# One hybrid encoder block: all big weights packed on the host in 8 KB pieces, full-row low parts of k, and projections emitted half a head sooner

## The chip, the cores and the metric

The kernel runs on one core of a Trainium2 chip. The metric is device time of one execution in microseconds (us); smaller is better. Repacking the weights is done with numpy before the launch and is not part of it.

## The reference, cut to what matters

Everything is float32. One sequence of 512 tokens, 1024 features, 16 heads of 64, 32 experts of width 512.

```
h = rmsnorm(x, norm_mix_g)
cb, cc, cu, q, k, v, f_logit, g_conv, g_att = split_cols(h @ w_in)     # w_in: 1024 x 8208
y_conv = short_conv(cb, cc, cu, conv_w, conv_b) @ w_conv_out
s = q k^T / sqrt(64) + cum[t] - cum[s]       # cum: running sum of log_sigmoid(f_logit + b_forget), causal
o = softmax(s) v                             # per head
m = sigmoid(g_conv) * y_conv + sigmoid(g_att) * (o @ w_att_out)
x = x + m @ w_out
x = x + hier_moe(rmsnorm(x, norm_ffn_g))     # best of 4 groups, then top 2 of its 8 experts
out = rmsnorm(x, norm_final_g)               # expert: (silu(h Wg) * (h Wu)) Wd
```

## The kernel before, in words

**Precision.** A float32 product is made of three fast TensorE products: both operands are split into a high part (a rounded copy, made by ACT) and a low part (the rest, made by DVE), and high x high, high x low, low x high are summed in PSUM. `mm3` (its matmuls are L120) does this over 8 blocks of 128 input features, 24 matmuls in all; `split` (L83 on ACT, L84 on DVE) makes the parts of a weight.

**Weights.** Projection weights come in column chunks of 256 (`CW`), 1 MB each. `load_raw` (L98) loads a chunk on SP's queue into one of two buffers (`wraw`), as `[128 partitions, 8 row blocks, 256 columns]`: each of a partition's eight pieces is 1 KB of DRAM, from another row of the weight. `split_w` then writes halves of the chunk into five buffers (`whl`). A `wraw` buffer is free for the next load when both halves are split, so each engine's queue and these two buffers set when a load starts.

**Stages.**
1. Start (written in the order of issue): x is normed and transposed into `hT`. The columns of v for the first four heads and the 16 of the forget gate come as two halves (`raw_v`, L245 and L246), q and k of these heads follow (`raws0`). The forget gates go through a chain of small DVE steps (`f_acc`), a transpose (`pf`, L391) and a running sum into DRAM (`ncd`), from where each head reads its row as `nct`.
2. Attention: per head `scores` (per block of 128 queries two products, L466 and L467, and a mask, L468; then DVE L469, the exponent on ACT L475), `transp` (L491) and `pvmm` (L507). Between heads, `gen_units` supplies 18 units of projection work (q, k, v of the next four heads; each 24 matmuls of 512 columns or the like) and `NSG` = 3 units of the attention gate (`pga`). A scheduler sets the order in each engine's queue from this program order. A pair of heads shares tiles: `q` holds for head r its own high part on the head's 64 rows and the low part on the other 64; `khi` holds the high part on both halves. `klo` holds the low parts of the pair, each on its own 64 rows, so L467 takes 64 of the 128 rows of both operands.
3. Merge: `gated` and the conv branch, all `mm3` with 512 columns; for the first `NSG` feature blocks the gate is already there.
4. Output projection (`px`), router and norm, woven by hand; `gain_rows` writes the normed tokens in a column order that suits the expert weights' rows, and they are stored in DRAM (`h2d`) and gathered by expert (`xg`).
5. Experts: gate and up (`pg`, L1022), down (`py`, L1037), combine (`pk`, L1063). Weights are loaded once each, 192 pieces of 1 MB, into 17 buffers (`prefetch`, L671) as buffers come free; a partition's piece is 8 KB of DRAM already, the next partition's lying 16 KB further.
6. Final norm and stores.

Of the kernel before, what the change touches and what calls it, by code (L numbers as in the profile page):

```python
# [13 lines left out]
F32 = mybir.dt.float32  # L14
F32R = mybir.dt.float32r
# [9 lines left out]
P = 128  # L25
T = 512
D = 1024
NK = D // P
# [16 lines left out]
def block_kernel(ctx, tc, x, norm_mix_g, w_in, conv_w, conv_b, b_forget, w_conv_out,  # L45
                 w_att_out, w_out, norm_ffn_g, w_router_group, w_router_expert,
                 w_e_gate, w_e_up, w_e_down, norm_final_g, out, dbg=None):
# [48 lines left out]
    def load_raw(src, name):  # L96
        raw = wraw.tile([P, NK, CW], F32, tag="wraw", name=f"raw_{name}")
        nc.sync.dma_start(raw, src.rearrange("(k p) f -> p k f", p=P))  # L98
        return raw

# [86 lines left out]
    qk = {}  # L187
# [7 lines left out]
    def qk_out(nm, pair, ps):  # L195
# [20 lines left out]
    def proj_qk(g):  # L216
        for nm, c0 in (("q", COL_Q), ("k", COL_K)):
            w = load_w(w_in[:, c0 + g * CW:c0 + (g + 1) * CW], f"{nm}{g}")
# [9 lines left out]
    with tc.tile_pool(name="s0", bufs=2) as s0:  # L228
# [6 lines left out]
        with tc.manual_schedule():  # L235
# [6 lines left out]
            for i in range(2):  # L242
                raw = p_tile(f"raw_v{i}")[:, 0:HK * VW].rearrange("p (k f) -> p k f", k=HK)
                src = w_in[i * T:(i + 1) * T].rearrange("(k p) f -> p k f", p=P)
                nc.sync.dma_start(raw[:, :, 0:CW], src[:, :, COL_V:COL_V + CW])  # L245
                nc.scalar.dma_start(raw[:, :, CW:VW], src[:, :, COL_F:COL_F + NH])  # L246
# [7 lines left out]
            raws0 = {nm: load_raw(w_in[:, c0:c0 + CW], nm + "0") for nm, c0 in (("q", COL_Q), ("k", COL_K))}  # L254
# [147 lines left out]
    NSG = 3  # L402
    sgp = opool.tile([P, NSG, T], F32, name="sgp")

    def gate_units():

        for fb in range(NSG):
            if fb % 2 == 0:
                w = load_w(w_in[:, COL_GA + fb * P:COL_GA + fb * P + CW], f"ga{fb}")
# [12 lines left out]
    with attx:  # L422
# [7 lines left out]
        def proj_v(g):  # L430
            w = load_w(w_in[:, COL_V + g * CW:COL_V + (g + 1) * CW], f"v{g}")
# [20 lines left out]
        def scores(h):  # L452
            pair, r = h // 2, (h % 2) * DH
            rows = slice(r, r + DH)
# [6 lines left out]
            for qb in range(NTB):  # L461
# [5 lines left out]
                nc.tensor.matmul(ps[:, :n], q[rows, h % 2, qs], kl[rows, :n], start=False, stop=False)  # L467
# [92 lines left out]
    if True:  # L560
        mT = (mga.tile([P, NK, T], F32R, name="mT_hi"), mga.tile([P, NK, T], F32R, name="mT_lo"))
        with tc.tile_pool(name="mg", bufs=2, side="right") as mg, \
# [7 lines left out]
            def gated(w_src, src, col, last):  # L570
                for c in range(D // CW):
                    ls = [lambda: load_w(w_in[:, col + c * CW:col + (c + 1) * CW], f"g{col}_{c}"),
# [801 lines left out]
```

## Time and profile before

| | us |
|---|---|
| median of 3 runs (1142.25 to 1765.85) | 1142.63 |
| profiled execution, its own time | 1140.45 |
| its span | 1138.9 |
| PE busy in the span | 1078.6 |
| DVE busy | 590.6 |
| ACT busy | 384.3 |

The profile covers one execution; its own time is the span and 1.5 us around it. The time of a matmul in it runs to a modelled end and overlaps the next one's, so the distance from start to start tells what one costs TensorE, and a high busy share doesn't mean that it never waits.

### The profile page before, as it was taken

The page shows a single profiled execution, that of the slowest core. Times are in us where ns is not written, and L with a number is a line of the kernel's source. Part 1 is how long each engine was busy: PE and PEld are TensorE (multiplying, and loading weights), DVE is VectorE, ACT ScalarE, POOL GpSimd, SP SyncE. Part 2 cuts the span into 40 slices and gives each one's busy share as a digit, 9 for nine tenths or more (in the row PEclk, how much of TensorE's full clock was granted, in tenths as well). Part 3 has the DMA queues.
Part 4 walks back from the last instruction along what each step waited for, and adds up shares of the span by engine and source line. Part 5 has one row for each costly group of instructions (what it writes and reads, how often), then busy time and mean ns, then how long its engine had stood idle before and what let it go on. Part 6 is the DMA issues. An engine that isn't in the chain of part 4 may idle for free.

```text
span 1138.9 us, 13609 instructions
## 1 busy us (share of the span) xinstructions
PE 1078.6 (95%) x5237; PEld 687.6 (60%) x5237; DVE 590.6 (52%) x1165; ACT 384.3 (34%) x726; POOL 53.1 (5%) x62
## 2 busy tenths in 40 slices
PE   6969999999999999999999799999999999999992
PEld 4747877687888888888899433333333333443441
DVE  6458776667422454433434425555555555445455
ACT  3436765567222333222342222222222222212222
POOL 4000000000200000000001200000000000000002
PEclk8989999999999999999999799999999999999996
DMA  7572343333755945555394799999999999999981
GB/s 206 61 117 65 68 81 72 59 74 59 134 124 82 105 93 95 94 99 125 107 361 166 298 389 419 419 418 419 419 418 419 419 419 420 418 418 419 419 341 76
DMA packets 83717, 268.07 MB, mean 235 GB/s; under 512 B 7104, under 2 KB 53232, under 8 KB 59072
## 3 DMA queue, kind: packets, MB, share of 16 engines
q1 hardware_dynamic: 76624, 255.34, 68.2%
q10 hardware_dynamic: 4224, 6.89, 1.9%
q0 software_dynamic: 2800, 4.93, 1.3%
q8 instruction: 42, 0.69, 0.2%
q14 instruction: 27, 0.22, 0.1%
HBM read 267.10 MB, written 4.23 MB: 238 GB/s over the span
## 4 chain that ended last, share of the span: by engine, by line
PE 84%; DMA 9%; DVE 3%; ACT 2%; issue 1%; DVEq 0%; SPq 0%; ACTq 0%
PE pg L1022 19%; PE py L1037 9%; PE py L120 8%; PE pg L120 6%; PE pk L1063 6%; PE px L120 4%; PE pb L120 4%; PE pu L120 4%; PE pc L120 4%; PE psv L120 3%; PE psq L120 2%; PE psk L120 2%; DMA raw_v<-in_w_in_dram 2%; PE s L467 2%; DMA raw_u<-in_w_e_up_dram 2%; DMA raw_d<-in_w_e_down_dram 2%
## 5 line engine op out<-in xcount | busy, mean ns | idle before, releaser
L1022 PE MATMUL pg<-raw_u,XT 128*64 128x512 f32 x512 | 235.1, 602 | 1.6 <-DMA raw_u<-in_w_e_up_dram 1.6
L1022 PE MATMUL pg<-raw_g,XT 128*64 128x512 f32 x512 | 236.1, 603 | 0.0
L1064 DVE TENSOR_TENSOR m<-pk,m 128x512 f32<-128x512 f32 x256 | 159.3, 684 | 137.6 <-PE pk L1063 137.5
L1022 PEld LDWEIGHTS pg<-raw_g,XT 128*64 128x64 f32 x512 | 64.9, 137 | 105.6 <-issue 102.7
L1037 PE MATMUL py<-raw_d,hTe 128*64 128x512 f32 x512 | 116.9, 598 | 0.0
L1047 DVE TENSOR_TENSOR Y<-py,Y 64x512 fp32r<-64x512 f32 x62 | 42.7, 688 | 75.8 <-ACT Y L1046 75.8
L1046 ACT ACTIVATE Y<-py 64x512 fp32r<-64x512 f32 x62 | 36.7, 592 | 125.3 <-PE py L1037 102.0
L1217 ACT ACTIVATE ta<-pg,rsl 64x512 f32<-64x512 f32 x32 | 21.9, 683 | 169.1 <-PE pg L1022 169.1
L1022 PEld LDWEIGHTS pg<-raw_u,XT 128*64 128x64 f32 x512 | 65.4, 137 | 21.0 <-issue 10.5
L1063 PEld LDWEIGHTS pk<-Y,S 128*128 128x128 f32 x248 | 41.7, 188 | 57.2 <-issue 49.5
L1063 PE MATMUL pk<-Y,S 128*128 128x512 f32 x248 | 74.6, 422 | 1.6 <-DVE Y L1047 1.6
L1037 PEld LDWEIGHTS py<-raw_d,hTe 128*64 128x64 f32 x512 | 34.0, 136 | 66.7 <-issue 59.7
L120 PE MATMUL pg<-hT_hi,whl_g 128*128 128x512 f32 x208 | 66.1, 389 | 0.0
L120 PE MATMUL px<-whl_o,mT_hi 128*128 128x256 f32 x256 | 47.9, 288 | 0.0
L120 PEld LDWEIGHTS pg<-hT_hi,whl_g 128*128 128x128 f32 x208 | 39.0, 188 | 8.1
L120 PE MATMUL psq<-hT_hi,whl_q 128*128 128x512 f32 x128 | 43.6, 408 | 0.0
L475 ACT ACTIVATE P<-P,mx 128x128 f32<-128x128 f32 (+1 forms) x64 | 35.2, 552 | 24.2 <-DVE mx L471 24.1
L120 PE MATMUL psk<-hT_hi,whl_k 128*128 128x512 f32 x128 | 42.8, 401 | 0.0
L469 DVE CUSTOM_DVE_ANT_0 P<-s,nct 128x128 f32<-128x128 f32 (+1 forms) x64 | 30.6, 489 | 22.4 <-PE s L468 17.7
L120 PE MATMUL py<-tT_hi,whl_y 128*128 128x512 f32 x128 | 40.7, 389 | 0.0
L120 PE MATMUL pg<-hT_lo,whl_g 128*128 128x512 f32 x104 | 40.5, 389 | 0.0
L120 PE MATMUL py<-oT_hi,whl_y 128*128 128x512 f32 x128 | 40.4, 389 | 0.0
(284 smaller groups left out, 1963.6 us busy)
## 6 DMA issues: line engine op xcount, KB each, us to landing
raw_g<-in_w_e_gate_dram SPq DMA_DIRECT2D x64, 1024.0 KB, 19.9
raw_u<-in_w_e_up_dram SPq DMA_DIRECT2D x64, 1024.0 KB, 19.9
raw_d<-in_w_e_down_dram SPq DMA_DIRECT2D x64, 1024.0 KB, 19.9
raw_g<-in_w_in_dram SPq DMA_DIRECT2D x7, 1024.0 KB, 11.7
raw_q<-in_w_in_dram SPq DMA_DIRECT2D x4, 1024.0 KB, 11.6
raw_k<-in_w_in_dram SPq DMA_DIRECT2D x4, 1024.0 KB, 13.6
nct<-ncd ACTq DMA_DIRECT2D x16, 256.0 KB, 3.2
raw_y<-in_w_att_out_dram SPq DMA_DIRECT2D x4, 1024.0 KB, 5.2
```

The lines of the kernel that those rows point to most:

```text
L120: nc.tensor.matmul(ps, blk(lhs[a], k, lsl), blk(rhs[b], k, rsl), start=i == 0, stop=i == 3 * NK - 1)
L467: nc.tensor.matmul(ps[:, :n], q[rows, h % 2, qs], kl[rows, :n], start=False, stop=False)
L469: nc.vector.tensor_tensor_reduce(Pt[:, P_OFF[qb]:P_OFF[qb] + kw], ps[:, :kw], nct[:, :kw], 1.0, NEG, ALU.add, ALU.max, mx[:, qb:qb + 1])
L475: nc.scalar.activation(Pt[:, sl], Pt[:, sl], AF.Exp, bias=mx[:, qb:qb + 1], accum_out=sm[:, qb:qb + 1])
L1022: nc.tensor.matmul(ps[r:r + DH], XT[:, k, j], w[k // 4][:, k % 4], start=k == 0, stop=k == NK - 1)
L1037: nc.tensor.matmul(py[n * DH:(n + 1) * DH], hTt[:, f], raws[f // 2][:, f % 2, n * T:(n + 1) * T], start=f == 0, stop=f == 3)
L1046: nc.scalar.activation(Y[hi, ns], py[hi], AF.Copy)
L1047: nc.vector.tensor_sub(Y[lo, ns], py[hi], Y[hi, ns].bitcast(F32))
L1063: nc.tensor.matmul(ps, S[:, tb * P:(tb + 1) * P], Y[:, ns], start=True, stop=True)
L1064: nc.vector.tensor_add(x2[:, tb, ns], ps, x2[:, tb, ns])
L1217: nc.scalar.activation(a, pg[0:DH], AF.Silu, scale=rsl[:, e:e + 1])
```

## The change

- `_pack` rearranges `w_in`, the three square weights and the expert weights with numpy: by chunk, partition and feature block, so that every 1 MB load is one run of DRAM in which each partition has one piece of 8 KB. The two first halves of v and the forget gate become one array `w_v0f`, a load each (4352 bytes a partition) with no second load on ACT's queue. The three expert arrays become one, `w_e`; its rows are in plain order, so `gain_rows` and `transpose_h` no longer permute columns.
- `klo` becomes two fixed tiles of `[128, 2, 512]`; the other head's 64 rows are set to zero once by POOL, and the product that was L467 (now L480) takes all 128 rows. A tile is written again by the pair after the next.
- `NSG` goes from 3 to 2: one gate unit moves from the attention into the merge, and the chunk that was loaded for it alone (`raw_ga2`) goes.
- `needed` emits the units that head h + 2 needs before `pvmm(h)`, where they stood before `scores(h + 1)` of the next turn.

```diff
     def load_raw(src, name):
         raw = wraw.tile([P, NK, CW], F32, tag="wraw", name=f"raw_{name}")
-        nc.sync.dma_start(raw, src.rearrange("(k p) f -> p k f", p=P))
+        nc.sync.dma_start(raw, src.rearrange("p (k f) -> p k f", k=NK))
         return raw
...
+    def klo_tile(pair):
+
+        if pair < 2:
+            t = klos[pair] = att.tile([P, 2, T], F32R, name=f"klo{pair}", bufs=1)
+            for r in range(2):
+                nc.gpsimd.memset(t[(1 - r) * DH:(2 - r) * DH, r].bitcast(F32), 0.0)
+        else:
+
+            assert 2 * (pair - 2) + 1 in scored
+        return klos[pair % 2]
...
-            kl = att.tile([P, T], F32R, tag="klo", name=f"klo{pair}", bufs=3)
+            kl = klo_tile(pair)
...
-                nc.vector.tensor_sub(kl[own], ps[own], kh[own, r].bitcast(F32))
+                nc.vector.tensor_sub(kl[own, r], ps[own], kh[own, r].bitcast(F32))
...
-                nc.sync.dma_start(raw[:, :, 0:CW], src[:, :, COL_V:COL_V + CW])
-                nc.scalar.dma_start(raw[:, :, CW:VW], src[:, :, COL_F:COL_F + NH])
+                nc.sync.dma_start(raw, w_v0f[i].rearrange("p (k f) -> p k f", k=HK))
...
-    NSG = 3
+    NSG = 2
...
-                nc.tensor.matmul(ps[:, :n], q[rows, h % 2, qs], kl[rows, :n], start=False, stop=False)
+                nc.tensor.matmul(ps[:, :n], q[:, h % 2, qs], kl[:, h % 2, :n], start=False, stop=False)
...
+        def needed(h):
+
+            return 6 * (h // 4) - (0 if h // 2 % 2 else 3) if 4 <= h < NH else 0
+
         scores(0)
         for h in range(NH):
 
             share = [NU * (2 * h + i) // (2 * NH) for i in range(2)]
             if h + 1 < NH:
-                g, odd = (h + 1) // 4, (h + 1) // 2 % 2
-                run_units(max(share[0], 6 * g - (0 if odd else 3) if g else 0))
+                run_units(max(share[0], needed(h + 1), 6 * (h // 4) - 1))
                 scores(h + 1)
             transp(h)
-            run_units(max(share[1], 6 * (h // 4) - 1))
+            run_units(max(share[1], needed(h + 2)))
             pvmm(h)
...
+        NBK = {"g": 4, "u": 4, "d": 2}
+
         def chunk_ap(part, n, i):
-
-            src = w_e_down if part == "d" else w_e_gate if part == "g" else w_e_up
-            return src[ORDER[n]].rearrange("(p i k) f -> i p k f", p=P, i=2)[i]
+            return w_e[ORDER[n], 2 * "gud".index(part) + i].rearrange("p (k f) -> p k f", k=NBK[part])
...
-            nc.tensor.transpose(pt[:, f], h.rearrange("t (p k) -> t k p", k=4)[:, f], identf[:DH, :DH])
+            nc.tensor.transpose(pt[:, f], h[:, f * P:(f + 1) * P], identf[:DH, :DH])
```

On PE, before the first score block of head 10 (`psk5` is the k projection of its pair, `t9`, `o9`, `o8` are transposes and PV products of heads 9 and 8, `psq6` the q projection of pair 6). Before:

```order
L120 MATMUL psk5_1776<-hT_hi_88,whl_k2_1_1482 128x512
L491 MATMUL t9_0_1844<-identf_60,P9_1654 128x128 x4
L491 MATMUL t9_1_1851<-identf_60,P9_1654 128x128 x3
L120 MATMUL psq6_1888<-hT_hi_88,whl_q3_0_1882 128x512
L120 MATMUL psq6_1888<-hT_lo_89,whl_q3_0_1882 128x512
L507 MATMUL o9_1866<-PThi1_615,v4_1597 128x512
...
L507 MATMUL o9_1866<-PTlo1_616,v4_1597 128x384
L466 MATMUL s10_0_1814<-khi5_1801,q5_1458 128x256
L467 MATMUL s10_0_1814<-klo5_1802,q5_1458 128x256
```

In the changed kernel, at the same place:

```order
L124 MATMUL psk5_1761<-hT_hi_88,whl_k2_1_1468 128x512
L520 MATMUL o8_1793<-PThi0_613,v4_1596 128x512
...
L520 MATMUL o8_1793<-PTlo0_614,v4_1596 128x256
L504 MATMUL t9_0_1842<-identf_60,P9_1706 128x128 x4
L504 MATMUL t9_1_1849<-identf_60,P9_1706 128x128 x3
L124 MATMUL psq6_1943<-hT_hi_88,whl_q3_0_1937 128x512
...
L479 MATMUL s10_0_1812<-khi5_1786,q5_1458 128x256
L480 MATMUL s10_0_1812<-klo1_596,q5_1458 128x256
```

The k projection now ends a PV product earlier: head 8's whole `pvmm` stands between it and the scores that read it, where four products of head 9's stood.

On POOL, after the store of the running sums (`ncd`) at the end of the start. Before:

```order
L338 TENSOR_TENSOR xt3_110<-xt3_110,gmix_111 128x1024
L393 MEMSET zero_552 16x512
L396 DMA ncd_103<-ncum_554 16x512
L565 IOTA ioti_2659 128x512
L692 DMA gcol_4399<-in_norm_ffn_g_dram 128x8x1
```

In the changed kernel:

```order
L406 MEMSET zero_550 16x512
L409 DMA ncd_103<-ncum_552 16x512
L198 MEMSET klo0_561 64x512 x2
L198 MEMSET klo1_596 64x512 x2
L582 IOTA ioti_2621 128x512
```

Four fills of 64 partitions by 512 elements are queued behind the store; the first `klo` product of head 0 and that of head 1 wait for POOL.

On SP's queue, where the attention ends and the merge begins (`y7184` and `g7184` are chunks of `w_att_out` and of the attention gate). Before:

```order
L98 DMA raw_v3_2188<-in_w_in_dram 128x8x256
L98 DMA raw_ga0_2479<-in_w_in_dram 128x8x256
L98 DMA raw_ga2_2589<-in_w_in_dram 128x8x256
L98 DMA raw_y7184_0_2663<-in_w_att_out_dram 128x8x256
L98 DMA raw_y7184_1_2723<-in_w_att_out_dram 128x8x256
```

In the changed kernel:

```order
L98 DMA raw_v3_2128<-in_w_in_dram 128x2048
L98 DMA raw_ga0_2511<-in_w_in_dram 128x2048
L98 DMA raw_y7184_0_2625<-in_w_att_out_dram 128x2048
L98 DMA raw_g7184_1_2685<-in_w_in_dram 128x2048
L98 DMA raw_y7184_1_2693<-in_w_att_out_dram 128x2048
```

`raw_ga2` is gone, and the shapes show one run of 2048 elements a partition in place of 8 of 256.

## Rows read from the trace of the kernel before

**Rows 1.** The page, section 4: the chain that ended last, by engine.

```profile
PE 84%; DMA 9%; DVE 3%; ACT 2%; issue 1%; DVEq 0%; SPq 0%; ACTq 0%
```

**Rows 2.** Stretches: length; busy PE, PEld, DVE, ACT, POOL; clock; DMA share; GB/s.

```profile
73.60:286.00 212.40, 207.11 (x1130) 161.32 (x1130) 151.59 (x386) 132.27 (x302) 1.47 (x2) 0.99 0.37 73
286.00:574.00 288.00, 288.00 (x1273) 238.46 (x1272) 115.82 (x145) 83.54 (x99) 4.85 (x8) 1.00 0.58 108
700.00:1000.00 300.00, 299.97 (x1354) 118.06 (x1350) 157.48 (x253) 71.21 (x126) 9.90 (x10) 1.00 1.01 419
```

**Rows 3.** The chain of waits in order of time: start us, us, what.

```profile
44.01 18.64 DMA raw_k<-in_w_in_dram
...
189.74 10.13 DMA raw_v<-in_w_in_dram
...
280.78 5.22 PE pga L120 x23
...
1005.57 20.57 DMA raw_d<-in_w_e_down_dram
```

**Rows 4.** DMA issues: queue, count, KB each, median us from issue to landing.

```profile
raw_k<-in_w_in_dram SPq DMA_DIRECT2D x4, 1024.0 KB, 13.6
...
raw_y<-in_w_att_out_dram SPq DMA_DIRECT2D x4, 1024.0 KB, 5.2
```

**Rows 5.** Timeline of the start, 38 to 78 us: start, length, engine, line.

```profile
62.68 1.06 ACT L83 ACTIVATE whl_k<-raw_k 128x1024 fp32r<-128x1024 f32 x1 [5.39 <-DMA raw_k<-in_w_in_dram]
...
66.33 1.02 PE L391 MATMUL pf<-identf,f_acc 128*16 128x128 f32 x4 [11.50 <-DVE f_acc L387]
```

**Rows 6.** Timeline of the first 25 us.

```profile
14.78 0.66 ACT L325 ACTIVATE PThi<-raw_v 128x544 fp32r<-128x544 f32 x1 [0.97 <-DMA raw_v<-in_w_in_dram]
...
17.37 4.65 POOL L338 TENSOR_TENSOR xt<-xt,gmix 128x1024 f32<-128x1024 f32 x2
...
17.46 2.27 DVE L146 SCALAR_TENSOR_TENSOR rs_t<-rs_y,rs_h 128x1 f32<-128x1 f32 x1
...
21.96 0.52 POOL L393 MEMSET zero<- 16x512 f32 x1
22.07 0.75 DVE L275 SCALAR_TENSOR_TENSOR xt<-xt,rstd,gmix 128x512 f32<-128x512 f32 x1
```

**Rows 7.** Timeline of PE, score blocks of one head.

```profile
150.26 0.36 PE L466 MATMUL s<-khi,q 128*128 128x256 f32 x1
150.55 0.38 PE L467 MATMUL s<-klo,q 64*128 64x256 f32 x1
150.86 0.23 PE L468 MATMUL s<-maskb,identb 128*128 128x128 bf16 x1
150.90 0.48 PE L120 MATMUL psq<-hT_hi,whl_q 128*128 128x512 f32 x1
...
151.89 0.47 PE L466 MATMUL s<-khi,q 128*128 128x512 f32 x1
152.29 0.50 PE L467 MATMUL s<-klo,q 64*128 64x512 f32 x1
152.73 0.23 PE L468 MATMUL s<-maskb,identb 128*128 128x128 bf16 x1
```

**Rows 8.** Timeline of PE, PV products of a head and a projection.

```profile
159.56 0.40 PE L507 MATMUL o<-PThi,v 128*128 128x512 f32 x1
159.80 0.40 PE L507 MATMUL o<-PTlo,v 128*128 128x512 f32 x1
...
161.31 0.28 PE L507 MATMUL o<-PThi,v 128*128 128x256 f32 x1
161.43 0.39 PE L120 MATMUL psk<-hT_lo,whl_k 128*128 128x512 f32 x1
```

**Rows 9.** Timeline, 195 to 206 us: what PE waits for at head 10.

```profile
199.89 1.06 ACT L83 ACTIVATE whl_v<-raw_v 128x1024 fp32r<-128x1024 f32 x1 [3.94 <-DMA raw_v<-in_w_in_dram]
...
201.61 0.39 PE L466 MATMUL s<-khi,q 128*128 128x256 f32 x1 [3.87 <-ACT khi L213]
```

More of the change, by code (lines that the diff above doesn't have):

```diff
@@ L97, in load_raw, with w_cols @@
         raw = wraw.tile([P, NK, CW], F32, tag="wraw", name=f"raw_{name}")
-        nc.sync.dma_start(raw, src.rearrange("(k p) f -> p k f", p=P))
+        nc.sync.dma_start(raw, src.rearrange("p (k f) -> p k f", k=NK))
         return raw
+    def w_cols(col):
+        return w_in[(col if col < COL_F else col - NH) // CW]
     def split_w(raw, name):
@@ L217, in proj_qk @@
         for nm, c0 in (("q", COL_Q), ("k", COL_K)):
-            w = load_w(w_in[:, c0 + g * CW:c0 + (g + 1) * CW], f"{nm}{g}")
+            w = load_w(w_cols(c0 + g * CW), f"{nm}{g}")
             for pair in (2 * g, 2 * g + 1):
@@ L253, in block_kernel @@
                 nc.sync.dma_start(xs[tb], x[tb * P:(tb + 1) * P])
-            raws0 = {nm: load_raw(w_in[:, c0:c0 + CW], nm + "0") for nm, c0 in (("q", COL_Q), ("k", COL_K))}
+            raws0 = {nm: load_raw(w_cols(c0), nm + "0") for nm, c0 in (("q", COL_Q), ("k", COL_K))}
             nc.scalar.dma_start(bfb, b_forget.rearrange("(o h) -> o h", o=1).to_broadcast([P, NH]))
@@ L408, in gate_units @@
             if fb % 2 == 0:
-                w = load_w(w_in[:, COL_GA + fb * P:COL_GA + fb * P + CW], f"ga{fb}")
+                w = load_w(w_cols(COL_GA + fb * P), f"ga{fb}")
             ps = psp.tile([P, T], F32, tag="proj", name=f"pga{fb}")
@@ L430, in proj_v @@
         def proj_v(g):
-            w = load_w(w_in[:, COL_V + g * CW:COL_V + (g + 1) * CW], f"v{g}")
+            w = load_w(w_cols(COL_V + g * CW), f"v{g}")
             v_tiles(g)
@@ L452, in scores @@
         def scores(h):
-            pair, r = h // 2, (h % 2) * DH
-            rows = slice(r, r + DH)
+            pair = h // 2
+            scored.append(h)
             q, (kh, kl) = qk["q", pair], qk["k", pair]
@@ L609, in block_kernel @@
                 for nm, col in (("c", COL_C), ("u", COL_U), ("b", COL_B)):
-                    w = load_w(w_in[:, col + c * CW:col + (c + 1) * CW], f"{nm}{c}")
+                    w = load_w(w_cols(col + c * CW), f"{nm}{c}")
                     for j in range(2):
@@ L739, in gain_rows @@
                 eng = nc.gpsimd if tb >= 2 else nc.vector
[L741 to L743 removed]
+                eng.tensor_mul(h2s[tb][:, c0:c1], x2[:, tb, c0:c1], gffn[:, c0:c1])
             def store_rows(tb):
@@ L1345, in block_kernel, with _pack, cols @@
             nc.sync.dma_start(out[tb * P:(tb + 1) * P], ot)
-_INS = ["x", "norm_mix_g", "w_in", "conv_w", "conv_b", "b_forget", "w_conv_out", "w_att_out", "w_out",
-        "norm_ffn_g", "w_router_group", "w_router_expert", "w_e_gate", "w_e_up", "w_e_down",
-        "norm_final_g"]
+_INS = ["x", "norm_mix_g", "w_in", "w_v0f", "conv_w", "conv_b", "b_forget", "w_conv_out", "w_att_out", "w_out",
+        "norm_ffn_g", "w_router_group", "w_router_expert", "w_e", "norm_final_g"]
 _OUTS = [((1, 512, 1024), "float32")]
+def _pack(inputs):
+    a = {n: np.asarray(v) for n, v in inputs.items()}
+    def cols(w):
+        return w.reshape(NK, P, -1, CW).transpose(2, 1, 0, 3).reshape(-1, P, NK * CW)
+    w = a["w_in"]
+    a["w_in"] = cols(np.concatenate([w[:, :COL_F], w[:, COL_GC:]], axis=1))
+    v0f = np.concatenate([w[:, COL_V:COL_V + CW], w[:, COL_F:COL_GC]], axis=1)
+    a["w_v0f"] = v0f.reshape(2, NK // 2, P, CW + NH).transpose(0, 2, 1, 3).reshape(2, P, NK // 2 * (CW + NH))
+    for n in ("w_conv_out", "w_att_out", "w_out"):
+        a[n] = cols(a[n])
+    a["w_e"] = np.concatenate([v.reshape(32, 2, v.shape[1] // 256, P, v.shape[2]).transpose(0, 1, 3, 2, 4)
+                               .reshape(32, 2, P, NK * CW) for v in (a["w_e_gate"], a["w_e_up"], a["w_e_down"])],
+                              axis=1)
+    return a
 def kernel(**inputs):
```

34 lines of the change are left out of this document (14 added, 20 removed).

## The prediction, made before the changed kernel ran

> **What bounds the kernel now.** I read the chain that ended last first: 84% of the span is PE and 9% DMA [rows 1], so each stage has to be asked what PE waits for there. The busy time by stretch comes next [rows 2]. In the merge PE is busy 288.00 of 288 us: its loads are hidden, whatever they cost. In the experts DMA is at 1.01 of its 16 engines and 419 GB/s for 300 us on end, and late in the stage the chain waits for `raw_d` [rows 3]: this stage ends when the stream of weights ends, and the stream starts when the stage before frees its buffers. The stage therefore moves as a block with whatever comes before it, and a faster TensorE inside it is worth nothing. In the attention PE shows 207.11 of 212.40 us, but starts, not ends, tell what a matmul costs, so the third view is the timeline of PE. The fourth is the chain in order of time, for the places where a load is waited for: `raw_k` for 18.64 us from 44.01 and `raw_v` for 10.13 us from 189.74 [rows 3].
>
> **The start: loads in 8 KB pieces.** A 1 MB chunk of `w_in` in 1 KB pieces lands after a median of 13.6 us, one of `w_att_out`, also in 1 KB pieces, after 5.2 [rows 4]. In the merge 0.58 of the DMA engines moves 108 GB/s, in the experts 1.01 moves 419 [rows 2]: 1 MB costs all engines 0.58 / 108 GB/s = 5.4 us there and 2.4 us here. The pieces of the experts are those that every weight gets now, so I take a landing between 2.4 us (that rate, no latency) and 5.2 us.
>
> From 38 to 67 us ACT splits chunks of the next group early; before `whl_k` it stands 5.39 us until that chunk lands [rows 5]. The splits are early work, but they stand in ACT's and DVE's queues ahead of the forget gates' small steps; these end 3.65 us after `raw_k` landed (62.68 to 66.33), and PE sits idle 11.50 us until then. `raw_k` is issued at 44.01, when its buffer is free. With 5.2 us it lands at 49.2 and `pf` could start at 49.2 + 3.65 = 52.9; PE gets there at 66.33 - 11.50 = 54.8 in any case. The whole wait of **11.5 us** goes, at either end of the landing, and what is late next is PE's own work.
>
> In the first 25 us ACT's split of the second half of v waits for its load until 14.78. Behind it POOL's two products with the gain run 4.65 us from 17.37, and DVE's tiny norm step beside them takes 2.27 us; the scaled second block of x, which PE waits for, starts at 22.07 [rows 6]. With v landing before 11, POOL's work starts up to 4.6 us sooner, and DVE's steps with it; but these still meet POOL's products, only earlier. Between 0 and 5 us; I take **3**, the middle, since half of DVE's delay is that meeting.
>
> **The attention: full-row low parts of k.** In a block of 256 columns L467 starts 0.29 us after L466 and L468 0.31 us after L467; with 512 columns it is 0.40 and 0.44 [rows 7]. A PV product with full rows and the same columns is followed by the next matmul after 0.12 us (256) and 0.24 us (512) [rows 8]. So each half-row product costs itself and its neighbour: 0.29 + 0.31 - 0.24 = 0.36 us in a small block, 0.40 + 0.44 - 0.48 = 0.36 in a large one. There are 16 heads x 4 blocks = 64 of them: 23 us. The mask product starts 0.04 us before its successor now (150.86 to 150.90, rows 7 again); alone, its 128 columns would cost half of 0.12, so about 0.02 us a block, or 1.3 us, comes back. **-21 us** with some rounding down for blocks whose L466 is fed late anyway. That the two rows stand apart only because of the 64 rows is an inference: operands, widths and clock are alike, and rows are what differs.
>
> The Trainium skill speaks on both sides here. "TensorE: Matmul & The Clock Gate", section "Why this matters for your kernels", says that a product with few rows takes the time of one with 128: by that, L467 loses nothing by its 64 rows, and the sum would be 21 us poorer. "TensorEngine Tiling (Array Packing)", section "Key Properties", says that a change of tiling mode drains the engine; by that the sum stands. The starts agree with the second: 0.29 and 0.31 us where 0.12 is had.
>
> Second term: at head 10 PE waits 3.87 us for `khi`, which stands in ACT's queue behind the split of `raw_v`, and that waited 3.94 us for its load [rows 9]. The load was issued at 189.74; with 5.2 us it lands at 194.9 in place of 199.9, and the wait goes. The granted clock over the attention is 0.99 [rows 2]; the 2.1 us (1% of 212.4) that this costs come from such waits, and most of it returns. **-5.4 us**.
>
> Third: the gate unit. 24 matmuls at 5.22 / 23 = 0.227 us [rows 3] leave the attention and stand in the merge, which PE bounds: -5.4 and +5.4, nothing. `raw_ga2` with its split goes with no one waiting for it.
>
> Fourth: what becomes late when PE is faster. DVE is busy 151.59 us and ACT 132.27 us of 212.4 [rows 2]; of a stage of 212.4 - 21 - 5.4 - 5.4 = 180.6 us DVE's work would be 84%. It is no bound by itself, but PE feeds two score buffers, and the next block must wait for DVE's pass over the block before the last. I put back 4 us: between 0, since the scheduler has projections to fill in, and 17 (below). The earlier emission works on the same account: the order shows head 8's whole PV product between k's projection and the scores of head 10, which covers ACT and DVE there; it is in the 4.
>
> The fills of `klo` on POOL stand behind the store of the running sums; a fill of 16 x 512 takes 0.52 us [rows 6], four make 2.1 us. PE's next work after `pf` is a k projection of 24 matmuls, 5.4 us, before any score reads `klo`: hidden. If `pf` came later than that projection they would cost up to 2.1 us. `klo`'s reuse waits for scores that stand more than one head earlier in PE's queue: nothing.
>
> **The experts.** Pieces stay 8 KB, now end to end. The stream already fills the engines, so I take 0. Its 192 pieces of 1.05 MB take 480 us at 419 GB/s; the 17 that fit ahead make 43 us of that, so 437 us have no cover, and bounds of 1% either way are 4 us. `gain_rows` and `transpose_h` in plain order act inside a stage that its stream bounds: 0.
>
> **How the numbers follow.** The profiled execution took 1140.45 us. Less 11.5, 3, 21 and 5.4, plus 4: 1140.45 - 36.9 = 1103.6 us. The median of the runs is 2.2 us above the profiled execution, so **1106 us**, 3.2% below the median. Verdicts at 2% start at 1119.8 us.
>
> **Rivals.**
> - DVE and ACT take over the attention (or the half rows are not the cause). For it: their busy share there grows from 71% to 84% of the stage, in queues that cannot skip ahead. Against it: PE is busy 207.11 of 212.40 us today [rows 2], and 3.87 of the rest are the one wait at head 10. Then the 21 us shrink to what they hide now; with 17 us given back, 1106 + 17 - 4 = **1119**; if the half rows cost nothing at all, 1106 + 21 - 4 = 1123.
> - The loads stay slow. `w_att_out` with 1 KB pieces lands in 5.2 us, so size alone isn't what makes `w_in` slow; it may be something that packing leaves. Then 11.5, 3 and 5.4 us stay where they are: 1106 + 19.9 = **1126**. Against it: the expert chunks have just this form and move at 419 GB/s. The Trainium skill, "DMA: Bandwidth & Descriptors", section "Specifications", puts the smallest transfer for full rate at 512 bytes: by it 1 KB pieces had nothing to gain. The share of 0.58 for 108 GB/s says otherwise.
> - Everything that waits goes too: no 4 us given back, 5 us in the first stretch, and the earlier emission removes short waits of PE before group changes, some 8 us: 1106 - 4 - 2 - 8 = **1092**.
> - The other side: the packed expert array streams more slowly than the three arrays did. The order of addresses can matter: chunks of `w_in` and `w_att_out`, equal in piece size, differ 13.6 to 5.2 us [rows 4]. With 437 us of stream uncovered, the 37 us gained are used up when it loses 37 / 437 = 8.5%; at 20%, which is far less than those two differ, it is 87 us longer, 1106 + 87 = **1193**. Against it: 1.01 of the engines for 300 us says that the engines, not the memory behind them, set the pace, and runs of 1 MB are not harder to read than pieces 16 KB apart.
>
> Chances: my forecast 0.58, DVE and ACT 0.19, slow loads 0.08, everything goes 0.11, slower stream 0.04. The range 1090 to 1122 takes in the first, most of the second and the fourth. About 2% is what a measurement of this kernel can tell from no change. Faster by more than that: 0.58 + 0.11, over half of the second (0.12) and a little of the third: 0.82. Slower: 0.03, as some of the last case stays near the median. The rest, 0.15, is the same.
>
> **What the new profile would show.** `pf` starts with no wait behind `raw_k`, before 55 us. `raw_k` and its like land in under 5.5 us. The starts of L479, L480 and L481 stand 0.12 to 0.13 us apart at 256 columns. The stretch from the first score to the last gate unit is near 186 us, DVE over 80% of it. The experts still run at 419 GB/s and as long as before. I would be wrong if the low product still starts 0.3 us after its neighbour, if PE waits for DVE between score blocks, or if the stream's rate is no longer 419.

## The result, and the profile after

The changed kernel takes **1111.95 us** (median of 4 runs, 1110.17 to 1112.66); the kernel before, on the same chip, 1144.66 (median of 4; one of them, of 1765.85, is far from every other and is left out of the ratio, which stands on the other three, 1142.25 to 1146.68). The ratio is 0.972, 95% interval [0.969, 0.975]: 2.8% faster. The forecast was 1106, its range 1090 to 1122. The profiled execution took 1110.17 us, its span is 1108.6; the sum of the prediction for that execution was 1103.6.

Stage by stage, between the same starts on PE in both timelines:

| From - to | before, us | after, us | change | predicted |
|---|---|---|---|---|
| span's start - first `psq` | 38.2 | 36.7 | -1.6 | -3 |
| first `psq` - `pf` | 28.1 | 16.5 | -11.7 | -11.5 |
| `pf` - first score | 7.3 | 5.9 | -1.4 | 0 |
| first score - first `py` of the merge | 212.2 | 190.3 | -21.9 | -27.8 |
| merge, to the first `px` | 288.3 | 294.7 | +6.4 | +5.4 |
| first `px` - end | 564.7 | 564.5 | -0.2 | 0 |
| sum | | | -30.3 | -36.9 |

The first row is one execution against one: in the nine runs whose start is that of the changed kernel the first `psq` comes between 36.6 and 37.7 us, 37.05 in the mean. Some 0.8 us of the merge's +6.4 come from the stage ahead of it: the granted clock is at its lower level, 1.2 GHz, from 247.8 to 251.1 us, behind the idle times of PE shown below, and the merge starts at 249.3. In experiment 4, without that idle time, the merge takes 293.9.

The windows of after stand beside [rows 2]: attention, merge, and 300 us of the experts (columns as there).

```profile
59.00:249.00 190.00, 183.66 (x1104) 153.42 (x1103) 146.96 (x379) 131.77 (x302) 0.00 (x0) 1.00 0.25 84
249.00:544.00 295.00, 295.00 (x1299) 244.24 (x1298) 116.50 (x150) 84.51 (x100) 6.34 (x9) 1.00 0.29 101
660.00:960.00 300.00, 298.30 (x1352) 117.72 (x1348) 157.56 (x253) 71.14 (x126) 10.87 (x11) 1.00 1.01 419
```

In the merge the DMA engines are taken for 0.29 of the time at 101 GB/s, where it was 0.58 at 108. The experts still stream at 419 GB/s. In the attention PE is idle for 6.3 us, and this idle time is in a new place. The landings, from the page's list of DMA issues (last number: median us), answer to [rows 4]:

```profile
raw_g<-in_w_in_dram SPq DMA_DIRECT2D x7, 1024.0 KB, 4.7
raw_k<-in_w_in_dram SPq DMA_DIRECT2D x4, 1024.0 KB, 5.5
...
raw_y<-in_w_att_out_dram SPq DMA_DIRECT2D x4, 1024.0 KB, 4.7
```

The chunks of `w_in` land in 4.7 (`raw_g`) and 5.5 us (`raw_k`, which took 13.6). At the start this does what [rows 5] let expect; here is the timeline of after around `pf`, ACT first, then PE:

```profile
48.36 1.05 ACT L83 ACTIVATE whl_k<-raw_k 128x1024 fp32r<-128x1024 f32 x1
...
52.88 0.39 PE L124 MATMUL psk<-hT_hi,whl_k 128*128 128x512 f32 x1
53.10 0.60 PE L404 MATMUL pf<-identf,f_acc 128*16 128x128 f32 x4
```

No row has a bracket, which would name a wait: nobody waits. PE comes to `pf` straight from a projection, and the four transposes take 0.60 us where they took 1.02 after the wait. The granted clock was 0.79 from `pf` to the first score before (66.3 to 73.6 us): its lower level, 1.2 GHz, until 69.3, behind PE's 11.5 us of idle time, and the upper one, 2.4 GHz, from there. It is 1.00 in that stretch now: that is the 1.4 us which the sum didn't have.

The first 25 us, for [rows 6]:

```profile
14.60 0.64 ACT L338 ACTIVATE PThi<-raw_v 128x544 fp32r<-128x544 f32 x1
...
15.14 1.04 ACT L279 ACTIVATE sq<-xt 128x1024 f32<-128x1024 f32 x1
...
16.09 0.19 ACT L279 ACTIVATION_READ_ACCUMULATOR sq<-xt 128x1 f32 x1
...
16.35 4.82 POOL L351 TENSOR_TENSOR xt<-xt,gmix 128x1024 f32<-128x1024 f32 x2 [1.94 <-DMA raw_q<-in_w_in_dram]
16.57 2.32 DVE L156 SCALAR_TENSOR_TENSOR rs_y<-rs_t,rs_y 128x1 f32<-128x1 f32 x1
18.93 2.26 DVE L150 SCALAR_TENSOR_TENSOR rs_t<-rs_y,rs_h 128x1 f32<-128x1 f32 x1
...
21.43 0.75 DVE L288 SCALAR_TENSOR_TENSOR xt<-xt,rstd,gmix 128x512 f32<-128x512 f32 x1
```

ACT's split of v no longer waits, but POOL's products begin only 1.0 us sooner (16.35 for 17.37). Before, they stood right behind POOL's own work on v, which ended at 17.41:

```profile
15.55 1.86 POOL L293 TENSOR_TENSOR PTlo<-raw_v,PThi 128x544 fp32r<-128x544 f32 x1
```

Now that work ends at 14.41, and POOL waits 1.94 us more. The bracket names `raw_q`, whose event came last, but the products don't read it. They overwrite blocks 2 and 3 of x, which had landed by 12.8 and 14.1 us; what ends just ahead of them, at 16.28, is ACT's square of block 2 (15.14, L279), which reads that block and stands in ACT's queue behind the split of v. DVE's one-column steps meet them as before, 2.3 us each, and the scale that PE waits for moves from 22.07 to 21.43.

The score blocks, for [rows 7], in the timeline of PE:

```profile
127.70 0.28 PE L479 MATMUL s<-khi,q 128*128 128x256 f32 x1
127.82 0.27 PE L480 MATMUL s<-klo,q 128*128 128x256 f32 x1
127.94 0.23 PE L481 MATMUL s<-maskb,identb 128*128 128x128 bf16 x1
127.98 0.36 PE L479 MATMUL s<-khi,q 128*128 128x256 f32 x1
128.18 0.28 PE L480 MATMUL s<-klo,q 128*128 128x256 f32 x1
128.30 0.23 PE L481 MATMUL s<-maskb,identb 128*128 128x128 bf16 x1
128.34 0.48 PE L124 MATMUL psq<-hT_hi,whl_q 128*128 128x512 f32 x1
128.66 0.34 PE L479 MATMUL s<-khi,q 128*128 128x384 f32 x1
128.84 0.33 PE L480 MATMUL s<-klo,q 128*128 128x384 f32 x1
129.02 0.23 PE L481 MATMUL s<-maskb,identb 128*128 128x128 bf16 x1
129.06 0.50 PE L479 MATMUL s<-khi,q 128*128 128x512 f32 x1
129.39 0.40 PE L480 MATMUL s<-klo,q 128*128 128x512 f32 x1
129.63 0.23 PE L481 MATMUL s<-maskb,identb 128*128 128x128 bf16 x1
```

After the low product the next start comes 0.12 us (256 columns) and 0.24 (512) later, as the PV products had it [rows 8]. After the high product it is 0.12 in the first block, but 0.20 and 0.33 where a mask stands directly ahead (127.98, 129.06). A projection behind a mask pays the same: from 128.34 it is 0.32 us to the next start, where 0.23 is usual. The distances from each score matmul to the next start, added up over 16 heads, are: before, 23.0 us behind the low products, 18.9 behind the high ones, 2.7 behind the masks; after, 10.6, 13.7 and 2.7. That is 44.6 - 27.0 = 17.6 us.

At head 10 ([rows 9]) nothing waits: `whl_v` is split at 187.55 with no idle time ahead of it. The idle time of after is at the end of the attention instead. First ACT, then PE, in the timeline:

```profile
232.41 0.59 ACT L525 ACTIVATE of<-o 64x512 f32<-64x512 f32 x1 [1.63 <-PE o L520]
233.02 1.28 ACT L425 ACT_TABLE_LOAD   x1
234.31 0.60 ACT L425 ACTIVATE sgp<-pga 128x512 f32<-128x512 f32 x1
...
235.58 1.28 ACT L488 ACT_TABLE_LOAD   x1
236.88 0.40 ACT L488 ACTIVATE P<-P,mx 128x128 f32<-128x128 f32 x1
...
240.05 1.28 ACT L425 ACT_TABLE_LOAD   x1
...
239.70 0.50 PE L520 MATMUL o<-PThi,v 128*128 128x512 f32 x1 [0.70 <-ACT PThi L507]
241.35 0.44 PE L504 MATMUL t<-identf,P 128*128 128x128 f32 x2 [1.14 <-DVE PTlo L508]
...
244.67 0.39 PE L520 MATMUL o<-PTlo,v 128*128 128x256 f32 x1 [0.91 <-DVE PTlo L508]
...
247.15 0.41 PE L504 MATMUL t<-identf,P 128*128 128x128 f32 x2 [1.53 <-DVE PTlo L508]
```

By starts (the distance from each matmul outside the score blocks to the next, less what it takes when PE is fed: about 0.227 us for 512 columns, 0.17 for 384, 0.12 for 256; so it counts the lower clock behind a wait too) the stalls of the attention were 12.1 us before, with 5.1 at head 10; they are 13.6 after, with 5.5 in the last ten us. The order of work names two suspects there. The last gate unit is used up at 238.6, so PE has nothing but heads 14 and 15 left. And ACT changes its table three times around head 15's exponents, because a gate's sigmoid now stands ahead of them.

### The profile page after: what moved, and what is told of

The parts are those of the page before. It is cut to its first block, busy times and chain, and to the rows that moved or that the text cites. A ratio compares the mean times of both kernels' runs of the same rounds, so it can differ in the third digit from the quotient of the medians.

```text
span 1108.6 us, 13613 instructions
## 1 busy us (share of the span) xinstructions
PE 1056.4 (95%) x5236; PEld 682.9 (62%) x5237; DVE 584.7 (53%) x1163; ACT 384.0 (35%) x726; POOL 55.1 (5%) x66
## 4 chain that ended last, share of the span: by engine, by line
PE 73%; DMA 21%; DVE 3%; ACT 2%; issue 1%; DVEq 0%; SPq 0%; ACTq 0%
DMA raw_u<-in_w_e_dram 13%; PE pg L1037 12%; PE py L124 8%; PE pg L124 7%; PE py L1052 6%; DMA raw_d<-in_w_e_dram 5%; PE px L124 4%; PE pu L124 4%; PE pc L124 4%; PE pb L124 4%; PE pk L1078 4%; PE psq L124 4%; PE psk L124 3%; PE psv L124 3%; PE o L520 2%; PE psv L314 1%
## 5 line engine op out<-in xcount | busy, mean ns | idle before, releaser
L1061 ACT ACTIVATE Y<-py 64x512 fp32r<-64x512 f32 x62 | 36.7, 591 | 125.5 <-PE py L1052 102.2
L124 PE MATMUL pg<-hT_hi,whl_g 128*128 128x512 f32 x224 | 71.2, 389 | 0.0
L124 PEld LDWEIGHTS pg<-hT_hi,whl_g 128*128 128x128 f32 x224 | 42.0, 188 | 8.7
L124 PE MATMUL pg<-hT_lo,whl_g 128*128 128x512 f32 x112 | 43.6, 389 | 0.0
L982 ACT ACTIVATE XT<-pxt 128x512 f32<-128x512 f32 x32 | 19.0, 595 | 61.8 <-PE pxt L981 61.8
L124 PE MATMUL pb<-hT_hi,whl_b 128*128 128x512 f32 x128 | 40.0, 389 | 0.0
```

Of the source, the lines that this page charges most:

```text
L124: nc.tensor.matmul(ps, blk(lhs[a], k, lsl), blk(rhs[b], k, rsl), start=i == 0, stop=i == 3 * NK - 1)
L982: nc.scalar.activation(XT[:, 4 * k4:4 * k4 + 4], pt, AF.Copy)
L1061: nc.scalar.activation(Y[hi, ns], py[hi], AF.Copy)
```

## The experiments

Each kernel is the changed one with the edit shown; ratios are to the kernel before on the same chip; where an edit has more lines than are shown, `...` marks the cut. The changed kernel stands at 0.972.

**1. The low product on 64 rows again (`e1_half_rows`).**

```diff
+            rows = slice(r, r + DH)
...
-                nc.tensor.matmul(ps[:, :n], q[:, h % 2, qs], kl[:, h % 2, :n], start=False, stop=False)
+                nc.tensor.matmul(ps[:, :n], q[rows, h % 2, qs], kl[rows, h % 2, :n], start=False, stop=False)
```

> The changed kernel with one part undone: the low product of the scores reads the head's own 64 rows of q and of k's low part again, instead of all 128 rows with zeros. My theory (the mixture of 64-row and 128-row products is what costs): the starts after the low product go back from .12, .18 and .24 to .31, .37 and .43 us, and the time rises by the 17.6 us that the score spacings of the two traces differ by, to about 1129 us. Rival (the packed loads brought the gain, the rows nothing): 1112 us, within 2 us of the changed kernel.

Measured: 1127.82 us, ratio 0.984 [0.979, 0.990], 15.9 us more than the changed kernel. The gaps behind the low products are 0.31, 0.37 and 0.43 us again, and first score to merge takes 206.3 us for 190.3. The rows are all that the edit changes, so they are what set the spacing: the inference of the prediction is shown. The Trainium skill, "TensorE: Matmul & The Clock Gate", section "Why this matters for your kernels", has a product with few rows take the time of a full one; here, between full-row products, it does not.

**2. `w_in` in rows again (`e2_w_in_rows`).** The halves of v come from the rows too, with the forget gate's columns as second loads; the square weights stay packed.

```diff
+        packed = src.shape[0] == P
...
-        nc.sync.dma_start(raw, src.rearrange("p (k f) -> p k f", k=NK))
+        if packed:
+            nc.sync.dma_start(raw, src.rearrange("p (k f) -> p k f", k=NK))
+        else:
+            nc.sync.dma_start(raw, src.rearrange("(k p) f -> p k f", p=P))
...
-        return w_in[(col if col < COL_F else col - NH) // CW]
+        return w_in[:, col:col + CW]
```

> The changed kernel with w_in alone read as before, row by row of the whole matrix: 1 KB pieces that stand 32.8 KB apart; square weights and experts stay packed. My theory (slow loads of w_in were the waits at the first products with f's weights and at head 10): both waits return, 11.7 us for the first, about 1.4 and 1.6 us beside it at the start, and 4 to 5 at head 10, some of which the later stalls take up: 1127 to 1131 us. Rival (the order of the emission or the split's place was the cause, not the loads): 1112 us.

Measured: 1139.69 us, ratio 0.995 [0.993, 0.998]: 27.7 us lost, well over what I expected. The first `psq` comes 2.3 us later, `pf` after a wait of 11.4, 11.5 more; the stretch behind it, at a granted clock of 0.80, costs 1.4. Another 13.4 us are in the attention. Its timeline of ACT has two waits for loads, and PE waits behind each, here behind the second:

```profile
187.02 1.06 ACT L83 ACTIVATE whl_v<-raw_v 128x1024 fp32r<-128x1024 f32 x1 [2.75 <-DMA raw_v<-in_w_in_dram]
...
246.33 1.06 ACT L83 ACTIVATE whl_g<-raw_g 128x1024 fp32r<-128x1024 f32 x1 [6.63 <-DMA raw_g<-in_w_in_dram]
...
248.67 0.58 PE L485 MATMUL s<-khi,q 128*128 128x256 f32 x1 [6.30 <-ACT khi L232]
```

The first is head 10's; PE waits 2.42 us there (189.36). The second is new: `raw_g`, the merge's first chunk of the attention gate, whose load is issued inside the attention, with its split in ACT's queue ahead of `khi` for head 14. In the kernel before this wait did not exist: there `raw_ga2` stood in the place of that load, and the merge's chunks of the attention gate were issued behind the attention, from 276.5 on.

**3. `w_in` by chunk, but in 1 KB pieces (`e3_w_in_1kb_runs`).**

```diff
-    a["w_in"] = cols(np.concatenate([w[:, :COL_F], w[:, COL_GC:]], axis=1))
+    a["w_in"] = np.concatenate([w[:, :COL_F], w[:, COL_GC:]], axis=1).reshape(D, -1, CW).transpose(1, 0, 2)
...
```

`load_raw` reads such a chunk row by row, as the kernel before did.

> The changed kernel with w_in packed by chunk, but inside a chunk still row by row: pieces of 1 KB, as before the change, though the whole chunk is 1 MB without gaps. It tells the size of the piece from the distance between pieces. If the distance (32.8 KB) made the loads slow: chunks land in about 5 us and the time is 1112 to 1114 us. If the 1 KB piece did: they land in about 13 us and the time is that of the kernel with w_in in rows, about 1128 us. I take the second at 6 in 10.

Measured: 1111.65 us, ratio 0.971 [0.965, 0.976], the time of the changed kernel. My bet on the piece was wrong. From the pages' lists of DMA issues, the row layout of experiment 2 and then this one:

```profile
raw_g<-in_w_in_dram SPq DMA_DIRECT2D x7, 1024.0 KB, 11.1
```

```profile
raw_g<-in_w_in_dram SPq DMA_DIRECT2D x7, 1024.0 KB, 5.7
```

The pieces are 1 KB in both. With 8208 floats, 32.8 KB, from one piece to the next the chunk lands in 11.1 us; end to end in 5.7; in pieces of 8 KB in 4.7. The share of the DMA engines between 290 and 540 us, in the same order, is 0.57 at 101 GB/s, 0.32 at 102, and 0.29 at 99. So the spread layout made the loads slow, and the size of the piece is worth one us a chunk. In that stretch the trace's packets of 1 KB take a median of 46 ns in both layouts, but a mean of 110 ns in rows and 53 end to end: it isn't that each piece is slow; 30% of them take over 100 ns, against 2%. `w_att_out` had shown it already: same pieces, 4 KB apart, 5.2 us [rows 4]. The Trainium skill, "DMA: Bandwidth & Descriptors", section "Latency and other measured facts", tells of copies that fall to about half rate when rows lie at pitches of large powers of two, and advises contiguous tiles; the pitches it measured begin at 512 KiB, and the 32,832 bytes here are no power of two, so it doesn't cover this loss. Nor does any run here separate the distance from the places where the pieces start: 32,832 is 32,768 + 64, so in rows the pieces no longer lie at multiples of 1 KB from the start of the array, and in the fast layouts they do. Which part of the path the time is lost in is not shown either.

**4. The emission as before (`e4_emit_old`).**

```diff
-                run_units(max(share[0], needed(h + 1), 6 * (h // 4) - 1))
+                g, odd = (h + 1) // 4, (h + 1) // 2 % 2
+                run_units(max(share[0], 6 * g - (0 if odd else 3) if g else 0))
...
-            run_units(max(share[1], needed(h + 2)))
+            run_units(max(share[1], 6 * (h // 4) - 1))
```

> The changed kernel with one part undone: the projections' chains of products are emitted half a head later, as before the change. My theory (with the loads fast and the splits early, the earlier emission is worth little): 1110 to 1116 us. Rival (the earlier emission is what removed the wait at head 10): a wait of 4 to 5 us of TensorE at head 10 or in the heads after it, and 1117 us or more.

Measured: 1105.95 us (1104.66 to 1106.07), ratio 0.965 [0.959, 0.971]; experiment 3 on the same chip took 1110.11 to 1112.94. Below either expectation: the sooner emission **costs** 6 us. No wait at head 10 comes back, so the packed loads alone removed it. First score to merge falls from 190.3 to 184.7, and the stalls from 13.6 to 8.0, the 5.5 in the last ten us to under 1. Gate products stand between the transposes and PV products of the last heads until 243.93, where the changed kernel's were used up at 238.6; and both heads' exponents come before the first sigmoid, so ACT loads one table there, not three:

```profile
233.53 0.19 ACT L488 ACTIVATION_READ_ACCUMULATOR P<-P,mx 128x1 f32 x1
...
235.39 1.28 ACT L425 ACT_TABLE_LOAD   x1
236.68 0.60 ACT L425 ACTIVATE sgp<-pga 128x512 f32<-128x512 f32 x1
```

**5. Rows and the old emission together (`e9_rows_emit_old`).** The edits of experiments 2 and 4.

> The changed kernel with two parts undone at once: w_in read row by row of the whole matrix, and the projections emitted half a head later. It tells whether the 28 us that the row layout alone took back are the loads' or come from the two together. Theory one (the loads cost some 20 us: about 14 at f's weights, 2 at the clock, 4 to 5 at head 10; the sooner emission makes late loads worse and costs 6 us beside them): about 1106 + 20 = 1126 us, and the 6.7 us wait for k's split near 242 us and the stall in the last heads are gone. Theory two (the two parts add up: 28 us for the loads whatever the emission): 1106 + 28 = 1134 us.

Measured: 1136.93 us, ratio 0.994 [0.991, 0.996]. Theory one falls, theory two is nearer: with slow loads the emission makes 2.8 us of difference, less than the spread of either kernel's runs (1134.48 to 1141.71 and 1135.23 to 1139.15), and slow loads cost 31 us over experiment 4. PE's stalls are 24.8 us, 19.2 of it in two places:

```profile
190.89 0.58 PE L485 MATMUL s<-khi,q 128*128 128x256 f32 x1 [4.03 <-ACT khi L232]
...
252.98 0.58 PE L485 MATMUL s<-khi,q 128*128 128x256 f32 x1 [8.06 <-ACT khi L232]
```

Behind each the clock is low (0.62 granted from 253 to 260 us), so the stretches of 20 and 30 us that hold them lose 7.4 and 11.8 us. This kernel has the full-row products, worth 17.6 us of starts, and yet its attention is only 10.8 us shorter than before, of which 5.4 are the moved gate unit: what the products gave, waits for `w_in` took back.

**6. The sigmoids of the gate units written behind the heads (`e5_sigmoid_late`).**

```diff
+    gates = []
...
-            nc.scalar.activation(sgp[:, fb], ps, AF.Sigmoid)
+            gates.append((fb, ps))
...
         run_units(NU)
+        for fb, ps in gates:
+            nc.scalar.activation(sgp[:, fb], ps, AF.Sigmoid)
```

> The changed kernel with the sigmoids of the two gate units that run under the heads put behind the head loop; the units stay in PSUM until then. My theory (the stall of TensorE of some 6 us in the last heads, at 238 to 249 us, comes from ScalarE changing between the tables of the sigmoid and of the exponent, 1.28 us each time, three times around head 15): two of the three loads leave the softmax of head 15, the time falls by 2 to 4 us to 1108 to 1110 us. Rival (what is missing there is a third gate unit as other work for TensorE, and the tables lie beside it): 1112 us, no change.

Measured: 1111.87 us, ratio 0.972 [0.971, 0.974]. This tells nothing of the theory: the scheduler put the sigmoids where they were, the table loads at 233.30, 235.86 and 240.32 for 233.02, 235.58 and 240.05.

**7. The gates' sigmoid by an exponent (`e10_gate_by_exp`).**

```diff
-            nc.scalar.activation(sgp[:, fb], ps, AF.Sigmoid)
+            nc.scalar.activation(sgp[:, fb], ps, AF.Exp, scale=-1.0)
+            nc.vector.tensor_scalar_add(sgp[:, fb], sgp[:, fb], 1.0)
+            nc.vector.reciprocal(sgp[:, fb], sgp[:, fb])
```

> The changed kernel with the sigmoid of the two gate units under the heads written as an exponent on ScalarE and a sum and a reciprocal on VectorE, so that no table is changed before the merge. (In the kernel with the sigmoids written later, they ran at the same place as before, so that it told nothing of the tables.) Theory of the tables (three loads of 1.28 us around head 15's softmax make the stall of 6 us in the last heads): the stall falls by 2.5 us or more, 1109 us or less. Rival (missing work for TensorE in the last heads makes the stall, since its softmax is longer than what is left of PE's own work): still over 5 us of stall, 1111 to 1113 us; VectorE's two added steps a unit may then even cost a us.

Measured: 1108.54 us, ratio 0.969 [0.967, 0.971], 3.4 us less; the stalls of the attention's last 20 us fall from 6.5 to 4.4. ACT goes from the gate to head 15's exponents without a load between:

```profile
233.49 0.60 ACT L425 ACTIVATE sgp<-pga 128x512 f32<-128x512 f32 x1 [0.36 <-PE pga L124]
...
235.88 0.40 ACT L490 ACTIVATE P<-P,mx 128x128 f32<-128x128 f32 x1
```

So the tables are worth two to three us of the new stall, as the theory had it, and not all of it. The rest isn't cleanly the missing work: the reciprocal takes DVE 3.34 us at 236.82, in the same heads.

**8. A third gate unit under the last heads (`e6_third_gate`).** It stays in PSUM until the merge.

```diff
-    NSG = 2
+    NSG, NSB = 3, 2
...
-            nc.scalar.activation(sgp[:, fb], ps, AF.Sigmoid)
+            if fb < NSB:
+                nc.scalar.activation(sgp[:, fb], ps, AF.Sigmoid)
+            else:
+                held[fb] = ps
...
```

> The changed kernel with a third gate unit run under the last heads, held in PSUM until the merge, so that TensorE has other work there and the merge one unit less. Theory of missing filler: the stall of some 6 us in the last heads is filled, the merge is shorter by the 5.4 us of a unit: about 1107 us. Rival (the loads of ScalarE's tables set the last heads' softmax, and the unit only lengthens the row of TensorE ahead of them): 1112 us.

Measured: 1104.41 us, ratio 0.966 [0.964, 0.968]. First score to merge takes 189.8 us with a unit more in it (190.3 without), and the merge 288.4 for 294.7. ACT still loads three tables (232.76, 235.32, 239.79), but PE's stalls are 7.6 us: it has work. So other work for PE is enough, with the tables as they are; experiment 4 has both cures, and 8.0 us of stalls.

**9. The gain products on DVE (`e8_no_pool_gain`).**

```diff
-            for tb in range(2, NTB):
-                nc.gpsimd.tensor_mul(xs[tb], xs[tb], gmix)
...
-            nc.scalar.activation(xs[3], xs[3], AF.Copy, scale=rstd[3])
+            scale_x(3, 0)
+            scale_x(3, 1)
```

> The changed kernel with the gain products of x blocks 2 and 3 moved from GpSimd to VectorE, in one operation with the scale, so that the two engines no longer meet on those blocks in the first 25 us. My theory (VectorE's steps of 2.3 us there are lengthened by GpSimd's products of 4.6 us): TensorE's first projection starts 3 to 4.5 us sooner, and the time is 1107 to 1109 us. Rival (the landing of the x blocks sets the start, and the split of the weights is as late): 1112 us.

Measured: 1107.10 us, ratio 0.968 [0.966, 0.970]. The steps that took 2.3 us beside POOL's products take a tenth of that, and the first `psq` starts at 32.02 for 36.65. In the timeline, DVE:

```profile
16.40 0.22 DVE L150 SCALAR_TENSOR_TENSOR rs_t<-rs_y,rs_h 128x1 f32<-128x1 f32 x1
16.66 0.16 DVE L156 SCALAR_TENSOR_TENSOR rstd<-rs_t,rs_y 128x1 f32<-128x1 f32 x1
16.85 0.75 DVE L288 SCALAR_TENSOR_TENSOR xt<-xt,rstd,gmix 128x512 f32<-128x512 f32 x1
```

The scale stands at 16.85, not 21.43: 4.6 us, and the time falls by 4.8.

**10. The experts' pieces 16 KB apart (`e7_experts_16kb`).**

```diff
-    return w_e[ORDER[n], 2 * "gud".index(part) + i].rearrange("p (k f) -> p k f", k=NBK[part])
+    return w_e[ORDER[n], "gud".index(part), :, i].rearrange("p (k f) -> p k f", k=NBK[part])
...
```

> The changed kernel with the experts' array packed so that the next partition's 8 KB piece lies 16 KB further and not 8 KB (the order of addresses inside an expert as before the change), same pieces, same number of transfers. My theory (a stream of 8 KB pieces runs at the same 419 GB/s in either order): 1112 us, within 2 us. Rival (the order of addresses sets the rate of the stream): the 474.3 us of the experts change by 1% or more, which is 4.7 us or more either way.

Measured: 1111.87 us, ratio 0.972 [0.970, 0.974]; from the experts' first product to PE's last instruction it is 474.4 us for 474.3. For pieces of 8 KB in this stream a distance of 16 KB costs nothing.

**11. No mask (`e12_no_mask`).** The mask product of every block is left out, so the output is another one.

```diff
-                nc.tensor.matmul(ps[:, :n], q[:, h % 2, qs], kl[:, h % 2, :n], start=False, stop=False)
-                nc.tensor.matmul(ps[:, qs], identb, maskb, start=False, stop=True)
+                nc.tensor.matmul(ps[:, :n], q[:, h % 2, qs], kl[:, h % 2, :n], start=False, stop=True)
```

> The changed kernel without the mask product of each block of scores; the softmax then reads unmasked scores on the diagonal block, and so the tokens and the experts' rows are others: only the attention's stretch and its starts are read, not the time. Theory one (the high product after the mask is followed late, 0.20 us at 256 columns where 0.12 is had, because of the bf16 product of the mask ahead of it): without it the high product's spacing falls to 0.12, 0.18 and 0.23 us, and TensorE's scores take 7 to 8 us less in all. Rival (the high product is followed late because it opens a new block, whatever ran before it): the spacing stays at 0.20, and 2.7 us less in all.

Measured: 1108.09 us, ratio 0.968 [0.965, 0.971], not read further. Two blocks that follow each other, in the timeline of PE:

```profile
59.16 0.28 PE L479 MATMUL s<-khi,q 128*128 128x256 f32 x1
59.27 0.28 PE L480 MATMUL s<-klo,q 128*128 128x256 f32 x1
59.39 0.28 PE L479 MATMUL s<-khi,q 128*128 128x256 f32 x1
59.51 0.28 PE L480 MATMUL s<-klo,q 128*128 128x256 f32 x1
```

The second block's high product is followed after 0.12 us, where it was 0.20 behind a mask. The median gaps are 0.12 and 0.24 us for 256 and 512 columns, so theory one has the cause: it is the mask product ahead. Whether by its type, bf16, or by its 128 columns, no run separates. It had the sum wrong: the scores' starts take 22.6 us for 27.0, 4.4 less and not 7 to 8, because not every high product follows a mask. Those with 384 columns (0.18 both times) mostly stand behind a projection, as at 128.66, and it is the projection that pays. The whole stretch is 4.6 us shorter.

**12. The best version: experiments 8 and 9 together (`e11_gate3_no_pool_gain`).**

> The third gate unit under the last heads and the gain products on VectorE, both at once, as the best version: the two gains lie in different stages (the last heads with the merge, 7.5 us; the first 25 us, 4.8 us). If they add up: 1111.9 less 12.3, about 1099.6 us, a ratio to the kernel before of 0.962. If the earlier start is lost again at a later load: 1103 to 1104 us.

Measured, in 5 runs: **1099.70 us** (1098.96 to 1100.81), ratio 0.961 [0.959, 0.963]. The gains add up to within 0.1 us.

## Why the prediction held, and where its terms were off

**The start: `pf` (11.5 us).** Right in place, mechanism and size: 11.7. Experiment 2 brings the wait back (11.4). What made the load slow I had left half open ("it may be something that packing leaves"); it was how the 1 KB pieces lay, 32.8 KB apart (experiment 3), which packing removes. So the 0.58 of the engines for 108 GB/s, which I read as the price of small pieces, was the price of this layout: end to end the same pieces take 0.32 for 102.

**The first 25 us (3 us).** Mis-sized, and the step behind it failed: "With v landing before 11, POOL's work starts up to 4.6 us sooner". It started 1.0 sooner: v's part did end 3.0 us sooner on POOL, but ACT's square of block 2, which ended at 17.18 before and at 16.28 now, was not in my rows, and POOL may not overwrite the block ahead of it. The half that I booked as left over, the meeting of DVE and POOL, is the real cost: experiment 9 takes 4.6 us from it.

**The clock (0).** A term that I didn't write down. The wait at `pf` left a granted clock of 0.79 behind, and 1.4 us went with it. That these 1.4 us make up for what the first 25 us fell short by is luck.

**The full rows (21 us).** Right in cause (experiment 1), mis-sized at 17.6 us of starts. The step was to price the high product at the PV products' spacing in every block; it keeps 0.08 us where a mask stands directly ahead (experiment 11).

**Head 10 (5.4 us).** Right: gone with the loads alone, as experiment 4 shows. What I did not see is how this term hangs on the one above. With slow loads (experiment 5) the faster attention runs into the same loads earlier, and into one more, `raw_g`, and gives 12.7 us of stalls back. That `raw_g` is issued inside the attention at all goes with the moved gate unit, which took `raw_ga2` out of the queue ahead of it; how much of the second wait is due to that, no run separates. The two parts are worth 15.9 and 27.7 us when each is undone alone; together that is more than the 32.2 that the whole change gains.

**Given back (4 us), with the emission inside it.** The step that failed is "The earlier emission works on the same account ... covers ACT and DVE there". It costs 6 us: the units are used up sooner, the last heads have no cover, and a sigmoid moves in ahead of head 15's exponents with three table loads around it (experiments 4, 7, 8). What I expected back from DVE did not come as a queue behind the score blocks; PE's stalls outside the last ten us are 8 us, where they were 7 before outside head 10. So stalls rose by 1.5 us (12.1 to 13.6) where -5.4 + 4 = -1.4 was predicted. DVE is busy for 77% of the attention (146.96 of 190.00 us), not over 80%.

**The gate unit (0).** +6.4 in the merge for +5.4, and about 5.4 out of the attention: right within 1 us, and most of that is the lower clock which the stall of the last heads leaves behind (293.9 us without it, in experiment 4). That the unit was also the last heads' cover, experiment 8 shows; kept there, it is worth 7.5 us together with its place out of the merge.

**The experts (0).** Right: the stretch from the first `px` to the end changed by 0.2 us, and moved as a block with what stands ahead of it. Experiment 10 closes the rival of the address order for 16 KB.

**Open.** How the part of the new stall that experiment 7 left divides between missing work and DVE's reciprocal; and what in the path of a load the layout in rows slows, by the distance of 32.8 KB or by where the pieces start.

## What to carry to other kernels

When two terms of a sum touch the same queue, a faster engine meets the loads earlier: price the second term in the schedule that the first one leaves, not in the trace of before. Work that only fills gaps is worth most in the last units of a stage, where nothing else is left to issue: before moving filler forward, ask what covers the tail. And look at how a load's pieces lie, not at their size alone.

## What the runs showed of the hardware that was not expected

- 1 MB in 1 KB pieces landed in 11.1 us with 32.8 KB between pieces and in 5.7 end to end; in 8 KB pieces in 4.7.
- A matmul on 64 rows among full-row ones cost 0.28 us: its own start to the next is 0.31 us for 0.12, and its full-row neighbour's 0.29 for 0.20. The bf16 mask product of 128 columns costs the product behind it 0.08 us.
- A one-column step of DVE took 2.3 us beside POOL's products of 128x1024, and 0.16 to 0.22 without them.
- ACT's change between exponent and sigmoid is a row of 1.28 us each way, with 0.01 to 0.02 us between it and the activations on either side: the one ahead ends at 233.00, the load starts at 233.02 and ends at 234.30, the next activation starts at 234.31. The Trainium skill, "ScalarE: Activation LUTs", section "What ACT_TABLE_LOAD costs", puts a drain of 1.38 us beside each load; these rows show no such time.
